# Two transformer blocks on one core: experts' norm applied in full, state-space evictions on ScalarE, four early expert units, rotation off Pool, cross-attention splits held to the softmax's end

## The chip, the cores and the metric

The program runs on one core of a Trainium2 chip. Its time is the device time of one execution in microseconds (us), the median of several. The engines are TensorE (PE, whose weight loads are shown apart as PEld), VectorE (DVE), ScalarE (ACT), GpSimd (POOL) and SyncE (SP, which issues most DMAs).

## What is computed

256 rows of 1024 float32 values pass through two blocks of two layers each, shortened from the reference:

```python
def first_block(x, ...):
    h = layer_norm(x, ln_in_g, ln_in_b)
    for l in range(2):
        mix = mixer_sublayer(h, ...)        # MLA + differential + forgetting attention, then w_out
        h = layer_norm(ALPHA * h + mix, ln1_g[l], ln1_b[l])
        ffn = grouped_moe(h, router_w, router_bias, w_gate[l], w_up[l], w_down[l])
        h = layer_norm(ALPHA * h + ffn, ln2_g[l], ln2_b[l])
    return h

def grouped_moe(h, ...):                    # 16 experts in 4 groups, best 2 of the best group
    scores = sigmoid(h @ router_w)
    ...
    for e in range(16):
        y = y + gates[:, e:e+1] * ((silu(h @ w_gate[e]) * (h @ w_up[e])) @ w_down[e])

def second_block(x, mem, ...):
    mem_k, mem_v = split(rms_norm(mem, mem_norm) @ mem_wkv, 2); mem_k = rms_norm(mem_k, mem_knorm)
    for i in range(2):
        x = x + 0.5 * swiglu(rms_norm(x, ffn1_norm[i]), ffn1_wi[i], ffn1_wo[i])
        h = rms_norm(x, mix_norm[i])
        x = x + (ssd_pool_mixer(h, ...) if i == 0 else swa_sink_attention(h, ...))
        x = x + memory_cross_attention(rms_norm(x, xattn_norm[i]), mem_k, mem_v, ...)
        x = x + 0.5 * swiglu(rms_norm(x, ffn2_norm[i]), ffn2_wi[i], ffn2_wo[i])
    return x
```

## The kernel before

The 256 rows are two tiles (`t` = 0, 1) of 128 partitions. Dense products are float32 by three passes (`mm3`, L483 to L485): each operand is split into a rounded high part and the rest, and high·high, high·low and low·high add up in PSUM. The experts' products (L1352 gate and up, L1386 down) and those of the memory (L1758) are single plain float32 passes.

**Weights.** `Stream` brings every weight once, in units of up to 1 MB, in the order of one list. A unit lands in one of two rings of tiles, `stage` (7) and `piece` (6). Dense weights are split on arrival, high on ACT (L161), low on DVE (L162); expert and memory units are "raw" and stay as they are. All these transfers are issued by SP, in order, each when its tile is free. Two expert units have places outside the rings, so that they can land before the experts begin: the first gate units of experts 0 and 1, in the main tiles `xl` and `m4`. `hold` and `go` keep splits of a named weight back and let some number of them go on.

**Order.** The program is laid out by a static scheduler: each engine gets one fixed list of instructions, formed from priorities, and `after(x)` keeps what follows behind `x`. So an instruction that waits holds up all behind it on its engine.

**The places that matter here.**
- *Norm before the experts* (`ln1`): a tile is normalised without its gain and bias (L581); they go into the router's weights (L1205, `rw`, `rc`), into the evictions of the gather (L1319 ACT, L1320 DVE) and, later, into the residual rows (`ln.gain`, L601 and L602). Each normalised tile is also split (L488 ACT, L489 DVE) for the gather.
- *Router*: transposes, 16 small matmuls (L1222), a sigmoid (L1225), some 20 small DVE instructions, then one-hot matrices (L1280) by which the rows of each expert are gathered with matmuls (L1318). Meanwhile PE runs one of the memory's products (L1758).
- *Experts*: eight pairs. Pair `pr` needs 8 gate and up units and 4 down units. Four groups of rows are gathered, group 0 ahead of the experts, group 1 in pair 0, groups 2 and 3 in pairs 2 and 4. `scatter` (L1401 on PE, L1403 on DVE) adds results to the rows. After the last pair, the next weights are split (4 of them, by `ws.go(4)`) and the second norm (`ln2`, L592 to L596) runs beside another product of the memory.
- *State-space mixer*: a four-tap convolution, decays, and per-head products; DVE evicts `upool` (L2059), `rows` (L2114), `bn` (L2145) and the gate `z` (L2189, a multiply out of PSUM).
- *Window attention*: key and value columns, then both halves of the queries, then the attention of the first half (scores L1980 and L1982, maxima L2000, exponentials, products), then that of the second.
- *Cross attention*: query product, norm of the queries, scores, softmax (L1831, L1841, L1856), products with the values, output product `xo`.

Of the kernel before, what the change touches and what calls it, by code (L numbers as in the profile page):

```python
# [16 lines left out]
P = 128  # L17
# [64 lines left out]
class Stream:  # L82
# [20 lines left out]
    def raw(self, key, ap, a, b, ring=0, slot=None):  # L103

        self.units.append(dict(ap=ap, a=a, b=b, left=1, tile=None, ring=ring, slot=slot, first=len(self.pieces)))
        u = len(self.units) - 1
        if not slot:
            self.use(key, u)
        return u

    def use(self, key, u):
        self.pieces.append(dict(key=key, u=u, raw=True, n=len(self.pieces)))

# [80 lines left out]
class LayerNorm:  # L194
# [8 lines left out]
    def tile(self, t):  # L203
        k = self.k
        if self.full:
            if t == 0:
                self.hi, self.lo = k.xt(self.tags[0]), k.xt(self.tags[1])
            k.ln_full(self.res, t, self.gb)
            self.copied = k.x_t(self.res[:, t, :], t, self.hi, self.lo, self.g)
            self.moved = k.moved  # L210
            return
        self.sqrt, self.last = k.ln_norm(self.res, t)
        if self.plain:
# [3 lines left out]
            if t == 0:  # L217
                self.hh = k.slot("m5", F32R).rearrange("p (t j f) -> p t j f", t=2, j=8)
                self.hl = k.slot("m2", F32R).rearrange("p (t j f) -> p t j f", t=2, j=8)
            v = self.res[:, t, :].rearrange("p (f j) -> p j f", j=8)  # L220
            self.parts = k.split(v, self.hh[:, t], self.hl[:, t])
        else:
            if t == 0:
                self.hi, self.lo = k.xt(self.tags[0]), k.xt(self.tags[1])
            self.copied = k.x_t(self.res[:, t, :], t, self.hi, self.lo, self.g, self.b)

# [41 lines left out]
class Kern:  # L268
# [62 lines left out]
    def plan(self):  # L331
        I, ws = self.I, self.ws
        for l in range(2):
# [11 lines left out]
            for c in range(2):  # L345
# [3 lines left out]
            early = lambda e, tag: ws.raw("gate", I["exp_w_gate"][l, e].rearrange("(p j) n -> p j n", j=8)[:, 0:4], 4, 512,  # L349
                                          slot=tag)  # L350
# [10 lines left out]

            def expert(key, ap, a, b):
                nonlocal n
                ws.raw(key, ap, a, b, n % (NSTAGE + NPIECE) % 2)
                n += 1

            for k in range(9):
                if k < 8:
                    for name in ("gate", "up"):
                        for j0 in (0, 4):  # L370
                            for e in (2 * k, 2 * k + 1):
                                if first:
                                    ws.use("gate", first.pop(0))
                                    continue
                                w = I["exp_w_" + name][l, e].rearrange("(p j) n -> p j n", j=8)
                                expert(name, w[:, j0:j0 + 4], 4, 512)
                if k > 0:
                    for c0 in (0, 2):
                        for e in (2 * k - 2, 2 * k - 1):
                            w = I["exp_w_down"][l, e].rearrange("(p c) n -> p c n", c=4)  # L380
                            expert("down", w[:, c0:c0 + 2], 2, 1024)
# [6 lines left out]
            mem(1024 * l + 512)  # L388
        self.plan2()

    def plan2(self):
        I, ws = self.I, self.ws
        for i in range(2):
# [15 lines left out]
            else:  # L409
                w = I["attn_wqkv_2"][0].rearrange("(p j) n -> p j n", j=8)  # L410
                self.plan_cols("qkv", w, 1024, 512)
                self.plan_cols("qkv", w, 0, 1024)
# [66 lines left out]
    def mm3(self, out, wst, wmv, first, last):  # L479
# [5 lines left out]
        return nc.tensor.matmul(out, al, bh, start=False, stop=last)  # L485
# [98 lines left out]
    def ln_full(self, res, t, gb):  # L584
# [10 lines left out]
        self.rsqrt1(r, mv[:, 1:2], 0)  # L595
        nc.vector.scalar_tensor_tensor(v, v, r, gb[1], op0=OP.mult, op1=OP.add)  # L596
# [221 lines left out]
    def mixer(self, l, norm, res, steps=None, moe=None):  # L818
# [182 lines left out]
        for k in range(2):  # L1001
            self.rope(qkd[:, k, :, :, 0:8], 4, 8, self.cos_d, self.sin_d, nc.gpsimd)
# [1289 lines left out]
```

## Time and profile before

| | |
|---|---|
| median of 3 runs (range) | 2002.53 us (2001.2 to 2002.54) |
| profiled execution | 2002.3 us |
| its span, first to last instruction | 2000.5 us |
| mean granted clock of TensorE, share of full speed | 0.986 |
| PE, PEld busy | 1935.0, 1458.6 us |
| DVE, ACT, POOL busy | 1127.0, 866.9, 58.0 us |
| moved by DMA | 453.39 MB, 227 GB/s over the span |

The span and the time differ by 1.8 us. PE is busy for 97% of the span, so at most 65.5 us of it are idle; the granted clock is 1 except in a few stretches, where the same matmuls take longer without PE being idle.

### The profile page before, as it was taken

To read this page: it belongs to the slowest core of one execution; us is meant where nothing else is said; L and a number is where in the kernel's file an instruction comes from. 1 tells how busy PE (TensorE), PEld (TensorE's weight loads), DVE (VectorE), ACT (ScalarE), POOL (GpSimd) and SP (SyncE) were. 2 spreads that over 40 slices of the span, in tenths; PEclk is the share of its full clock that TensorE was granted. 3 is DMA by queue.
4 is the path that set the end of the run, shared out by engine and by line. 5 is a ranking of instruction groups with operands and counts; after the bars stand their busy time and mean duration, and the time that the engine had idled before them with its cause. 6 is when DMAs were issued, how large, how long until landed. Compare 5 with 4: busy or idle time off the path is not lost.

```text
span 2000.5 us, 28009 instructions
## 1 busy us (share of the span) xinstructions
PE 1935.0 (97%) x11069; PEld 1458.6 (73%) x11069; DVE 1127.0 (56%) x2211; ACT 866.9 (43%) x1539; POOL 58.0 (3%) x119
## 2 busy tenths in 40 slices
PE   6999999999999998899999899999999999999999
PEld 6776433367864333599988887899989986778998
DVE  7775122167751221656579775655665567766554
ACT  6563110136631101455466555644454455556443
POOL 1110000000100000000001000000000000000000
PEclk9999999999999999999999999999999997999999
DMA  8456999973569999855564353455555543335550
GB/s 290 145 203 229 397 419 420 421 256 123 206 236 403 420 421 421 300 187 181 186 202 137 132 219 109 163 190 190 190 200 186 182 165 137 127 99 175 190 190 22
DMA packets 176044, 453.39 MB, mean 227 GB/s; under 512 B 11120, under 2 KB 106844, under 8 KB 149148
## 3 DMA queue, kind: packets, MB, share of 16 engines
q1 hardware_dynamic: 172044, 435.55, 59.1%
q0 software_dynamic: 3856, 15.91, 2.2%
q8 instruction: 91, 1.49, 0.3%
q14 instruction: 53, 0.43, 0.1%
HBM read 446.19 MB, written 5.24 MB: 226 GB/s over the span
## 4 chain that ended last, share of the span: by engine, by line
PE 56%; DMA 5%; DVE 3%; ACT 2%; issue 0%; POOL 0%; DVEq 0%; SPq 0%; POOLq 0%; ACTq 0%
PE mm L1623 7%; PE mm L1625 7%; PE mm L1624 7%; PE accb L485 5%; PE accb L484 5%; PE accb L483 4%; PE acca L485 4%; PE acca L484 4%; PE acca L483 4%; DMA piece<-in_exp_w_gate_dram 2%; DMA piece<-in_exp_w_down_dram 1%; DMA stage<-in_exp_w_down_dram 1%; DMA stage<-in_exp_w_up_dram 1%; DVE piece L162 1%; PE mm L1876 1%; PE mm L541 1%
## 5 line engine op out<-in xcount | busy, mean ns | idle before, releaser
L162 DVE TENSOR_TENSOR piece<-stage,piece 128x1024 fp32r<-128x1024 f32 (+3 forms) x439 | 513.8, 1179 | 240.9 <-ACT piece L161 239.3
L161 ACT ACTIVATE piece<-stage 128x1024 fp32r<-128x1024 f32 (+3 forms) x439 | 444.5, 1021 | 343.8 <-PE mm L1625 204.4
L1352 PE MATMUL mm<-stage,m 128*64 128x512 f32 x512 | 221.8, 595 | 0.0
L1352 PE MATMUL mm<-piece,m 128*64 128x512 f32 x480 | 215.1, 596 | 2.0 <-DMA piece<-in_exp_w_up_dram 2.0
L1623 PE MATMUL mm<-m,piece 128*128 128x256 f32 x736 | 207.0, 281 | 2.3 <-DVE m L2189 2.3
L1624 PE MATMUL mm<-m,piece 128*128 128x256 f32 x736 | 206.7, 281 | 0.0
L1625 PE MATMUL mm<-m,piece 128*128 128x256 f32 x736 | 206.6, 281 | 0.0
L1623 PE MATMUL mm<-xh,piece 128*128 128x256 f32 x576 | 163.1, 283 | 0.0
L1625 PE MATMUL mm<-xh,piece 128*128 128x256 f32 x576 | 163.0, 283 | 0.0
L1624 PE MATMUL mm<-xl,piece 128*128 128x256 f32 x576 | 162.9, 283 | 0.0
L484 PE MATMUL accb<-piece,m 128*128 128x512 f32 (+1 forms) x364 | 144.3, 397 | 0.0
L485 PE MATMUL accb<-piece,m 128*128 128x512 f32 (+1 forms) x364 | 143.7, 395 | 0.5 <-DVE m L493 0.5
L483 PE MATMUL accb<-piece,m 128*128 128x512 f32 (+1 forms) x364 | 143.1, 394 | 0.9 <-ACT m L950 0.7
L1623 PEld LDWEIGHTS mm<-m,piece 128*128 128x128 f32 x736 | 139.4, 189 | 4.6 <-issue 3.0
L1624 PEld LDWEIGHTS mm<-m,piece 128*128 128x128 f32 x736 | 139.3, 189 | 1.9 <-issue 0.3
L1625 PEld LDWEIGHTS mm<-m,piece 128*128 128x128 f32 x736 | 139.4, 189 | 0.0
L483 PE MATMUL acca<-piece,m 128*128 128x512 f32 (+1 forms) x348 | 138.2, 398 | 0.2
L485 PE MATMUL acca<-piece,m 128*128 128x512 f32 (+1 forms) x348 | 137.2, 396 | 0.5 <-DVE m L493 0.5
L484 PE MATMUL acca<-piece,m 128*128 128x512 f32 (+1 forms) x348 | 137.7, 396 | 0.0
L1352 PEld LDWEIGHTS mm<-stage,m 128*64 128x64 f32 x512 | 65.1, 137 | 76.4 <-issue 73.8
L1623 PEld LDWEIGHTS mm<-xh,piece 128*128 128x128 f32 x576 | 110.4, 192 | 1.3
L1624 PEld LDWEIGHTS mm<-xl,piece 128*128 128x128 f32 x576 | 110.4, 192 | 1.2
(567 smaller groups left out, 3535.8 us busy)
## 6 DMA issues: line engine op xcount, KB each, us to landing
stage<-in_ffn_wi_dram SPq DMA_DIRECT2D x88, 1024.0 KB, 5.5
stage<-in_ffn_wo_dram SPq DMA_DIRECT2D x44, 1024.0 KB, 5.4
stage<-in_exp_w_down_dram SPq DMA_DIRECT2D x38, 1024.0 KB, 18.6
stage<-in_exp_w_up_dram SPq DMA_DIRECT2D x34, 1024.0 KB, 11.2
stage<-in_exp_w_gate_dram SPq DMA_DIRECT2D x30, 1024.0 KB, 18.5
piece<-in_exp_w_gate_dram SPq DMA_DIRECT2D x30, 1024.0 KB, 17.9
piece<-in_exp_w_up_dram SPq DMA_DIRECT2D x30, 1024.0 KB, 15.0
piece<-in_exp_w_down_dram SPq DMA_DIRECT2D x26, 1024.0 KB, 16.8
```

The lines of the kernel that those rows point to most:

```text
L161: nc.scalar.activation(wh, src, AF.Copy)
L162: nc.vector.tensor_tensor(wl, src, wh.bitcast(F32), op=OP.subtract)
L483: nc.tensor.matmul(out, ah, bh, start=first, stop=False)
L484: nc.tensor.matmul(out, ah, bl, start=False, stop=False)
L485: return nc.tensor.matmul(out, al, bh, start=False, stop=last)
L541: self.moved = nc.tensor.transpose(p[:, k * P:(k + 1) * P], src[:, 4 * q + k:D:8], self.c["ident"])
L1352: mm = nc.tensor.matmul(o[64 * k:64 * k + 64, :], x[:, j, s:s + CAP], w[k][:, jj, :], start=(j == 0), stop=(j == 7))
L1623: nc.tensor.matmul(out, wh[:, j, :], hi[:, j, :], start=(j == 0), stop=False)
L1624: nc.tensor.matmul(out, wh[:, j, :], lo[:, j, :], start=False, stop=False)
L1625: nc.tensor.matmul(out, wl[:, j, :], hi[:, j, :], start=False, stop=(j == 7))
L1876: nc.tensor.matmul(po[:, k * P:(k + 1) * P], v[:, mc, h * 256 + cc * P:h * 256 + (cc + 1) * P], pt[t][:, (2 * h + mc) * P:(2 * h + mc + 1) ...
```

## The change

Seven edits, put in together:

1. `ln1` applies gain and bias at once (`ln_full`, two DVE passes of a tile, L594 and L596 of before). The premultiplied router weights, their bias row, the later `ln.gain`, and the row loads for it go; the gather's evictions become plain copies. Both tiles are split after the second one's norm.
2. Four expert units instead of two have places of their own (`xl`, `m4`, `m1`, `xh`), and they are other units, of later use: an up unit of expert 0 and three down units. The gathers of groups 1, 2 and 3 move to the end of pair 1 and into pairs 3 and 5. The second half of the memory's weights stands ahead of the next dense weight in the list.
3. The splits at the experts' end come later: two after the first tile of `ln2` is transposed, the rest after the second.
4. The rotation of the differential attention's queries and keys runs on DVE instead of POOL.
5. `upool`, `rows` and `bn` are evicted on ACT; `z` is copied out by ACT and multiplied by DVE in SBUF.
6. Cross attention finishes its query product bank by bank, starts the norm of each bank at its end, and puts the transposes and scores behind the last matmul; the splits of `xo` wait for the last normalised probabilities.
7. Window attention takes the first half of the queries, then keys and values, then the attention of the first half, then the second half of the queries.

```diff
-            first = [early(0, "xl")]
+            slots = {("up", 0, 4): "m4", ("down", 0, 0): "xl", ("down", 1, 0): "m1", ("down", 0, 4): "xh"}
...
+            early("down", 0, 0)
             self.plan_rows("w_out", I["w_out"][l].rearrange("(c p) n -> p c n", p=P), 8)
-            first.append(early(1, "m4"))
+            early("up", 0, 4)
...
+                    if n == NSTAGE + NPIECE - 2:
+                        early("down", 1, 0)
+                        early("down", 0, 4)
+            mem(1024 * l + 512)
...
-            mem(1024 * l + 512)
...
-            self.rope(qkd[:, k, :, :, 0:8], 4, 8, self.cos_d, self.sin_d, nc.gpsimd)
+            self.rope(qkd[:, k, :, :, 0:8], 4, 8, self.cos_d, self.sin_d, nc.vector)
...
-        ln = LayerNorm(self, res, ("ln1", l), None, ("xh",), plain=True)
+        ln = LayerNorm(self, res, ("ln1", l), self.load_gb(I["ln1_g"], I["ln1_b"], l), ("xh",), plain=True, full=True)
...
-                nc.tensor.matmul(o, n[:, j, t * P:(t + 1) * P], self.rw[l][:, j, :], start=False, stop=(j == 7))
+                nc.tensor.matmul(o, n[:, j, t * P:(t + 1) * P], self.rw[:, j, :], start=(j == 0), stop=(j == 7))
+        ws.free.append("xh")
...
-        at = gather(0)
-        with self.after(at):
-            ln.gain(rows)
+        gather(0)
...
-                if pr == 8:
-                    with self.after(state["silu"], state["tr"]):
-                        ws.go(4)
-            if pr == 0:
-                gather(1)
...
+            if pr == 1:
+                gather(1)
...
                 nxt.tile(0)
+            with self.after(*nxt.copied):
+                ws.go(2)
...
+        ws.hold("xo")
+        self.gemm_rows("xq", 8, lambda k: (hi[:, k, :], lo[:, k, :]), acc=rows(), done=chain, cuts=(2,), by_bank=True)
+        with self.after(self.last_mm):
+            for x in steps:
+                next(x, None)
...
+        with self.after(at[3]):
+            ws.go()
...
-        queries(0, 1)
+        attend(0, bias, "xl")
         queries(1, 1)
-        attend(0, bias, "xl")
...
-                nc.vector.tensor_scalar(u[:, t, b * 512:(b + 1) * 512], acc[t], r[:, t:t + 1], None, op0=OP.mult)
+                nc.scalar.activation(u[:, t, b * 512:(b + 1) * 512], acc[t], AF.Copy, scale=r[:, t:t + 1])
...
-            nc.vector.tensor_tensor(zs[:, ch, :], p[:, 0:256], rrow, op=OP.mult)
+            nc.scalar.activation(zs[:, ch, :], p[:, 0:256], AF.Copy)
+            nc.vector.tensor_tensor(zs[:, ch, :], zs[:, ch, :], rrow, op=OP.mult)
```

**Order on PE, first attention of the window layer.** Before: `accb` collects the last of the query product (high parts `m_16266`, low `m_16267`), `acca` the scores, `xh` holds normalised queries, `prob` probabilities.

```order
L485 MATMUL accb<-piece,m_16267 128x512
L1980 MATMUL acca<-m_16394,m_16392 128x128 x2
L1982 MATMUL acca<-m_16394,m_16392 128x256 x2
L1980 MATMUL acca<-m_16394,m_16392 128x128 x2
L1982 MATMUL acca<-m_16394,m_16392 128x256
L1967 MATMUL mm<-ident,xh 128x128 x8
L1982 MATMUL acca<-m_16394,m_16392 128x256
```

The same place after the change (`m_16227` and `m_16228` are the high and low parts, L1968 transposes keys, L1981 and L1983 are the scores):

```order
L1968 MATMUL mm<-ident,m_16354 128x128 x8
L487 MATMUL accb<-piece,m_16227 128x512
L488 MATMUL accb<-piece,m_16227 128x512
L489 MATMUL accb<-piece,m_16228 128x512
L1981 MATMUL acca<-m_16355,m_16353 128x128 x2
L1983 MATMUL acca<-m_16355,m_16353 128x256 x2
L487 MATMUL accb<-piece,m_16227 128x512
L488 MATMUL accb<-piece,m_16227 128x512
L1981 MATMUL acca<-m_16355,m_16353 128x128
L1983 MATMUL acca<-m_16355,m_16353 128x256
```

The scores of the first half, which came when the query product was over, now stand among the matmuls of the second half's queries.

**Order on DVE, end of the first layer's experts.** Before: the scatter's additions to `res`, splits of the next weight (L162) and the second norm (L592 on).

```order
L489 TENSOR_TENSOR xh<-acca,xh 128x512
L162 TENSOR_TENSOR piece<-stage,piece 128x768 x2
L489 TENSOR_TENSOR xh<-acca,xh 128x512
L162 TENSOR_TENSOR piece<-stage,piece 128x768 x2
L1403 SCALAR_TENSOR_TENSOR res<-res,mm 128x512 x4
L592 BN_STATS bnst<-res 128x6 x3
```

After the change:

```order
L494 TENSOR_TENSOR xh<-accb,xh 128x512 x2
L1387 SCALAR_TENSOR_TENSOR res<-res,mm 128x512 x4
L494 TENSOR_TENSOR xh<-acca,xh 128x512 x2
L1387 SCALAR_TENSOR_TENSOR res<-res,mm 128x512 x4
L597 BN_STATS bnst<-res 128x6 x3
```

No split stands between the scatter's additions and the norm any more.

**Order on DVE, the norm ahead of the router, second tile.** Before: norm (L581), split of that tile (L489), copy of the transposed tile that the router reads (L565, `xh`), and the router's first instruction.

```order
L531 TENSOR_TENSOR lnr<-sq_y,sq_t 128x1
L581 TENSOR_SCALAR res<-res,bnmv,lnr 128x1024
L489 TENSOR_TENSOR m_1639<-res,m_1638 128x1024
L565 COPY xh<-mm 128x4x128
L1227 TENSOR_TENSOR gbi<-gsc,rb 128x32
```

After the change:

```order
L536 TENSOR_TENSOR lnr<-sq_y,sq_t 128x1
L601 SCALAR_TENSOR_TENSOR res<-res,lnr,gv 128x1024
L494 TENSOR_TENSOR m_1686<-res,m_1685 128x1024 x2
L570 COPY xh<-mm 128x4x128
L1215 TENSOR_TENSOR gbi<-gsc,rb 128x32
```

The split of the first tile, which ran while the second was being summed, now stands with the other ahead of the router's copy.

## Rows read from the trace of the kernel before

**Rows 1.** PE's waits, experts of layer 0: what for, us in total, times, longest.

```profile
PE mm L1401 <- DVE res L1403: 2.9, 4, 1.8
...
PE mm L1352 <- DMA piece<-in_exp_w_up_dram: 1.3, 1, 1.3
```

**Rows 2.** PE's waits, experts of layer 1.

```profile
PE mm L541 <- DVE sq_y L530: 4.0, 1, 4.0
PE accb L1386 <- DMA stage<-in_exp_w_down_dram: 2.1, 2, 1.3
PE accb L1758 <- DMA stage<-in_mem_wkv_dram: 1.4, 1, 1.4
```

**Rows 3.** Stretches: length, busy PE, PEld, DVE, ACT, POOL, granted clock, DMA share, GB/s.

```profile
175.00:200.00 25.00, 25.00 (x147) 16.04 (x147) 11.34 (x21) 7.56 (x12) 1.09 (x2) 0.93 0.46 147
...
375.00:400.00 25.00, 21.73 (x91) 7.47 (x88) 3.88 (x7) 3.28 (x5) 0.28 (x3) 1.00 1.01 421
```

**Rows 4.** Stretches at the experts' ends, layers 0 and 1.

```profile
412.50:417.50 5.00, 4.65 (x8) 2.35 (x9) 5.00 (x10) 0.30 (x1) 0.00 (x0) 0.66 1.07 373
...
822.50:827.50 5.00, 4.34 (x13) 3.01 (x14) 3.81 (x12) 4.07 (x11) 0.00 (x0) 0.66 1.07 385
```

**Rows 5.** Timeline of DVE, end of layer 0's experts: start, us, line, operation.

```profile
408.04 1.83 DVE L162 TENSOR_TENSOR piece<-stage,piece 128x768 fp32r<-128x768 f32 x2
...
416.97 1.27 DVE L594 SCALAR_TENSOR_TENSOR res<-res,bnmv,gv 128x1024 f32<-128x1024 f32 x1
```

**Rows 6.** PE's waits from the state-space mixer to the cross attention.

```profile
PE tp L2175 <- DVE prob L2166: 3.4, 2, 2.3
PE mm L1623 <- DVE m L2189: 2.3, 1, 2.3
PE mm L1837 <- DVE m L1831: 1.6, 1, 1.6
```

**Rows 7.** Stretches of the state-space mixer.

```profile
1075.00:1100.00 25.00, 24.99 (x162) 19.71 (x161) 23.82 (x57) 14.96 (x23) 5.28 (x6) 1.00 0.29 98
...
1112.50:1120.00 7.50, 5.24 (x34) 4.88 (x30) 5.83 (x12) 1.58 (x4) 0.00 (x0) 0.54 0.63 225
```

**Rows 8.** Timeline of DVE, end of the state-space mixer.

```profile
1109.52 1.22 DVE L162 TENSOR_TENSOR piece<-stage,piece 128x1024 fp32r<-128x1024 f32 x1
...
1111.78 1.41 DVE L2059 TENSOR_SCALAR m<-accb,rms_r 128x512 f32<-128x512 f32 x2
```

**Rows 9.** PE's longest wait in the window layer.

```profile
PE acca L1980 <- DVE wnm L2000: 4.5, 2, 4.2
```

**Rows 10.** Stretches of the window layer: query projection, attention's first half, its second half.

```profile
1650.00:1665.00 15.00, 15.00 (x70) 12.31 (x69) 14.34 (x25) 8.00 (x10) 0.53 (x1) 1.00 0.76 262
1677.00:1703.00 26.00, 25.24 (x85) 16.03 (x85) 12.95 (x69) 12.19 (x44) 0.00 (x0) 0.50 0.08 32
1703.00:1719.00 16.00, 16.00 (x91) 10.05 (x89) 11.20 (x60) 7.74 (x29) 0.00 (x0) 0.99 0.01 2
```

**Rows 11.** Timeline of DVE, norm ahead of the router, layer 0.

```profile
162.67 0.81 DVE L581 TENSOR_SCALAR res<-res,bnmv,lnr 128x1024 f32<-128x1024 f32 x1
165.62 2.02 DVE L489 TENSOR_TENSOR m<-res,m 128x1024 fp32r<-128x1024 f32 x1 [2.15 <-ACT m L488]
```

**Rows 12.** Timeline of ACT, same place and the gather.

```profile
161.76 1.28 ACT L504 ACT_TABLE_LOAD   x1
163.06 0.20 ACT L504 ACTIVATE warm<-eps 128x1 f32<-128x1 f32 x1
...
169.44 0.20 ACT L1225 ACTIVATE gsc<-tp 128x32 f32<-128x32 f32 x1 [3.26 <-PE tp L1222]
176.12 0.56 ACT L1319 ACTIVATE m<-mm,gcol 128x256 f32<-128x256 f32 x1 [6.49 <-PE mm L1318]
```

**Rows 13.** Groups of instructions, 100 to 106 us: busy us, mean ns.

```profile
L1205 PE MATMUL tp<-rw,gcol 128*1 128x16 f32 x32 | 1.1, 176 | 0.0
```

**Rows 14.** The rotation's line 771: count, duration in ns least/median/most.

```profile
L771 DVE TENSOR_TENSOR m<-gv x2: 425/425/425, 67.4 to 472.1; 128x256 f32<-128x256 f32 x2
```

More of the change, by code (lines that the diff above doesn't have):

```diff
@@ L103, in raw @@
     def raw(self, key, ap, a, b, ring=0, slot=None):
-        self.units.append(dict(ap=ap, a=a, b=b, left=1, tile=None, ring=ring, slot=slot, first=len(self.pieces)))
+        first = max((p["n"] + 1 for p in self.pieces if not p.get("raw")), default=0)
+        self.units.append(dict(ap=ap, a=a, b=b, left=1, tile=None, ring=ring, slot=slot, first=first))
         u = len(self.units) - 1
@@ L204, in tile @@
         k = self.k
[L205 to L212, printed above, removed]
+        self.sqrt, self.last = k.ln_full(self.res, t, self.gb) if self.full else k.ln_norm(self.res, t)
         if self.plain:
@@ L217, in tile @@
             if t == 0:
[L218 to L221, printed above, removed]
+                return
+            self.hh = k.slot("m5", F32R).rearrange("p (t j f) -> p t j f", t=2, j=8)
+            self.hl = k.slot("m2", F32R).rearrange("p (t j f) -> p t j f", t=2, j=8)
+            with k.after(self.sqrt, self.last):
+                for i in range(2):
+                    v = self.res[:, i, :].rearrange("p (f j) -> p j f", j=8)
+                    k.split(v, self.hh[:, i], self.hl[:, i])
         else:
@@ L797, in block1 @@
         self.ws.start(5)
-        next(moe)
+        self.moe_consts()
         self.ws.start()
@@ L808, in block1 @@
         for l in range(2):
-            ln = self.mixer(l, ln, res, *([] if l else [steps, moe]))
+            ln = self.mixer(l, ln, res, *([] if l else [steps]))
             if self.stop == 1 + 2 * l:
@@ L816, in block1, with mixer @@
         return res, ln
-    def mixer(self, l, norm, res, steps=None, moe=None):
+    def mixer(self, l, norm, res, steps=None):
         nc, I, c, ws = self.nc, self.I, self.c, self.ws
@@ L1210, in moe @@
         n, hh, hl = ln.n, ln.hh, ln.hl
-        x = self.slot("m1")
-        rows = [x[:, 0:D], x[:, D:2 * D]]
-        for r, v in zip(rows, (I["ln1_g"], I["ln1_b"])):
-            nc.gpsimd.dma_start(r, bcast_rows(v, D, l * D))
+        ws.free.append("m1")
         sc = self.sm(32, "gsc")
@@ L1357, in gate_or_up @@
                 ws.release(2)
+            state["last"] = mm
             return o
@@ L1842, in queries, with chain @@
                          nc.vector.tensor_scalar(qv[:, :, 1, :], pv[:, :, 1, :], g[:, 1:2], None, op0=OP.mult))
-            sc[t] = [self.acc(t), self.acc(t)]
-            for h in range(4):
-                for cc in range(2):
-                    nc.tensor.matmul(sc[t][h // 2][:, (h % 2) * 256:(h % 2) * 256 + 256], qT[:, 2 * h + cc, ts[t]],
-                                     kT[:, 2 * h + cc, :], start=(cc == 0), stop=(cc == 1))
+            for b in banks:
+                s = self.acc(t)
+                sc.setdefault(t, []).append(s)
+                for h in range(2):
+                    for cc in range(2):
+                        nc.tensor.matmul(s[:, h * 256:h * 256 + 256], qT[:, 4 * b + 2 * h + cc, ts[t]],
+                                         kT[:, 4 * b + 2 * h + cc, :], start=(cc == 0), stop=(cc == 1))
+        normed, steps = [], []
+        def chain(*x):
+            steps.append(queries(*x))
+            next(steps[-1])
         def attend(t):
```

200 lines of the change are left out of this document (93 added, 107 removed).

## The prediction

> **What bounds the kernel now.** I read the page first: PE is busy for 1935.0 of 2000.5 us, so the edits can win back only the 65.5 us in which it is idle and the stretches in which its clock is low; its own work hardly changes. Then the waits of PE and the table of stretches, stage by stage, for where these lie. Four places carry most of what the diff touches.
>
> *Experts.* In the later pairs DMA is the limit: its share is 1.01 at 421 GB/s, and PE is idle for 3.27 of 25 us (25.00 - 21.73) [rows 3]. A unit of 1 MB (1.049 million bytes) takes 2.49 us at that rate. PE waits for weights at single places: 1.3 us in layer 0 [rows 1], 2.1 us and, for the memory's weights, 1.4 us in layer 1 [rows 2].
>
> *Experts' ends.* DVE makes four splits ahead of the last additions to `res`, the first two 1.83 us [rows 5]. PE waits up to 1.8 us for `res` in layer 0 [rows 1] and 4.0 us for the second norm in layer 1 [rows 2], and in either layer a stretch of 5 us has a mean clock of 0.66 [rows 4], that is, part of it at 1.2 GHz.
>
> *State-space mixer.* DVE is busy for 23.82 of 25 us [rows 7]; PE then waits 3.4 and 2.3 us for it [rows 6], and has a mean clock of 0.54 for 7.5 us [rows 7].
>
> *Window attention.* PE waits 4.2 us for a maximum on DVE [rows 9], and its clock is at 0.50, the 1.2 GHz level, for the next 26 us, the whole first half. PE counts as busy there; the same work of the second half takes 16 us at 0.99 [rows 10].
>
> **The change part by part.** The sum is made against the profiled execution, 2002.3 us, which is 0.2 under the median of the three runs.
>
> *Early units.* Between 175 and 200 us DMA's share is 0.46 [rows 3], so some 13.5 us of it stand free: the rings are full, and no tile is released before the experts begin. Two more units outside the rings take 2 × 2.49 = 5.0 us from that free time, and all later weights arrive 5.0 us sooner. The three shown waits for weights (1.3 + 2.1 + 1.4 = 4.8 us) go. SP issues in order, so if it stood at `xh`, which comes free only after the router's matmuls, the units behind it would stand too; they need ring tiles that come free later still. Lower end: nothing, if PE's pace and DMA's are so close that the wait comes back in a later pair. Upper end: all of the 3.27 us of the late stretch [rows 3] in both layers and 1.4 for the memory, 8. I take **5**.
>
> *Gathers later.* Group 1 is gathered at the end of pair 1, and pair 2's gate product needs it: its last eviction of 0.56 us [rows 12] may stand open there, once in a layer. Groups 2 and 3 stay a product ahead. 0 to -2, I take **-1**.
>
> *Experts' ends.* Without the splits on DVE, the norm of layer 0 comes some 3.6 us sooner (two times 1.83 [rows 5]). To win: the waits of 1.8 [rows 1] and 4.0 us [rows 2], and what the low clock costs, 5 × (1 - 0.66) = 1.7 us in either layer [rows 4]: 9.2 at most. The splits now stand after the transposes, where DVE needs about 0.9 us for each; the next dense product can be held by the third and fourth. Lower end 2, I take **6**.
>
> *Norm in full, router.* 32 small matmuls in the records (16 instructions) go, 1.1 us [rows 13], under full load of PE: **1**. On the chain to the router, L581 (0.81 us [rows 11]) becomes a pass like L594 (1.27 [rows 5]), and the first tile's split now stands before the router's copy, 2.02 us on DVE [rows 11]. DVE had waited 2.15 us for ACT at that place [rows 11], so the added split partly fills a wait; by that the sigmoid, now at 169.44 [rows 12], comes some 2.0 to 2.5 us later. The cover is the memory's product; where it ends, PE waits. The four bias matmuls and 9 us of `ln.gain` on DVE that go were hidden under it. I take **-1.5** for both layers, with -5 (all 2.5 us in each) and 0 as ends.
>
> *Rotation.* 12 instructions in each layer, at most 0.425 us each on DVE (a row of four times the width [rows 14]), 5.1 us at most, under dense products and on a DVE that is nearly idle there: **0**.
>
> *State-space evictions.* `upool` leaves DVE with 1.41 us for two of its four [rows 8], so 2.8 in all, `rows` and `bn` with a little more. For `z` DVE keeps a multiply of the same size, and only its wait for PE moves to ACT, which was busy for 1.58 of 7.5 us [rows 7]. To win: waits of 5.7 us [rows 6], and the low clock, 7.5 × (1 - 0.54) = 3.4 us [rows 7], 9 together; lower end 1, because `prob` on DVE (L2166) stays behind a split of 1.22 us [rows 8]. I take **5**, what the shorter DVE list explains and a part of the clock.
>
> *Cross attention.* The query chain of one bank lies under the other's matmuls: the wait of 1.6 us [rows 6], which the second layer shows too, 3.2 together, 5 with smaller ones. Against it, the `xo` splits begin only when the probabilities are normalised; if two of 1.22 us [rows 8] are late in each layer, that is -5. I take **2.5**.
>
> *Window attention.* The second half's queries stand among the scores of the first half, so PE has a dense product to run while DVE and ACT do the softmax. If the first half goes like the second, 26 us become 16 [rows 10], and the 4.2 us [rows 9] go as well: 14.2. ACT must change its table twice more between exponentials and a square root: 2 × 1.28 us [rows 12] = 2.6, on a chain that PE waits for. DVE also gets the second half's splits and norms. Ends 0 (the clock stays low) and 17 (4.2 and half of 26). I take **10**.
>
> A rule speaks against the last step. The Trainium skill (ScalarE: Activation LUTs, "What ACT_TABLE_LOAD costs") gives 2.66 us for a change of table, the load and a drain behind it. This trace disagrees: the ACTIVATE at 163.06 starts 0.02 us after the load has ended [rows 12]. By the page the two changes would cost 5.3 us in place of 2.6, and the sum would be 2.7 us smaller.
>
> Sum: 5 - 1 + 6 + 1 - 1.5 + 0 + 5 + 2.5 + 10 = 27; 2002.3 - 27 = 1975.3, so **1975 us**.
>
> **The rivals.**
> *The window attention keeps its low clock in the first half.* For it: PE, DVE and ACT hand each head pair on, and the clock stayed at 0.50 through all of it [rows 10]. Against it: the second half, which is made of the same steps, ran at 0.99. Then only the wait of 4.2 is won, less 2.6: 1975 + 10 - 1.6 = 1983 us.
>
> *The experts give nothing and the router takes its upper price.* The waits for weights come back in later pairs (0 for 5), and the chain ends 2.5 us late in each layer (-5 for -1.5): 1975 + 5 + 3.5 = 1984 us.
>
> *Slower.* The projection that now fills the first half is drawn into the low clock with it: PE has gaps while it waits for DVE, the clock is at 0.50 from the first score to the last, the second half too. Then the first half wins nothing (10), the second takes 32 in place of 16 us [rows 10] (16), and the projection, 48 matmuls (8 weight chunks, 2 tiles, 3 passes) at 15.00 / 70 = 0.214 us [rows 10], takes 20 in place of 10 us (10): 1975 + 36 = 2011 us. It decides when 27 of these 36 us come about.
>
> *Better.* All ends of experts' tails, mixer and window come in: 1975 - 3 - 4 - 7 = 1961 us.
>
> **How the numbers follow.** Forecast 58% (1966 to 1982 for itself), low clock in the first half 17%, experts and router 12%, slower 6%, better 7%. The first three and a part of the better one hold 8 in 10 and more between 1962 and 1984 us; the upper end of 1992 is for the splits of `xo`, which could cost 7.5 us more than I took. A measurement of this kernel tells about 0.2%, 4 us, from no change: faster than 1998.5 us is 0.90, between that and 2006.5 is 0.04 (the rivals of smaller gain together), slower 0.06.
>
> **What the profile after would show.** Early units: no wait for expert or memory weights, DMA's share in the stretch before the experts above 0.46. Ends: `res` additions without a split before them, no wait on the norm in layer 1, clock 1 there. Mixer: PE's waits on L2166 and `z` shorter, clock near 1 up to 1120. Window: granted clock 1 through the first half, no wait of some 4 us, the stage 10 us shorter. Router: the sigmoid some 2 us later after the norm, PE's wait there under 1.5 us. Wrong it would be if the clock of the window attention stayed at 0.50, if PE waited for `xo` pieces in both layers, or if the gather of group 1 held up pair 2 by more than a microsecond.

## The result

The changed kernel took 1955.57 us (median of four runs, 1954.59 to 1958.93) against 2002.53; the ratio is 0.977 with a 95% interval of 0.9753 to 0.9787. That is 47 us, where 27 were forecast, and 6 us under the low end of the range. The profiled execution took 1954.59 us, its span is 1952.8.

The page of the changed kernel, busy time of each engine (us, share of the span, instructions):

```profile
PE 1910.2 (98%) x11029; PEld 1445.3 (74%) x11029; DVE 1121.6 (57%) x2236; ACT 866.1 (44%) x1558; POOL 46.7 (2%) x93
```

PE is idle for 42.6 us (1952.8 - 1910.2) where it was idle for 65.5, and its busy time fell by 25 us, although it lost only 40 short records: most of that part is time at the low clock. The mean clock rose from 0.986 to 0.997, so the span lost some 28.0 us to the low clock before (2000.5 × 0.014) and 5.9 after (1952.8 × 0.003), an estimate that counts idle time at the low clock too.

The waits of PE of the changed kernel, whole span (us in total, times, longest):

```profile
PE mm L546 <- DVE res L586: 7.2, 1, 7.2
...
PE mm L1152 <- DVE prob L2017: 3.7, 2, 3.1
PE mm L546 <- DVE sq_y L535: 2.6, 2, 1.3
...
PE acca L1370 <- DMA piece<-in_exp_w_down_dram: 0.3, 1, 0.3
```

Of the waits in [rows 1, 2, 6, 9], those for expert weights are down to 0.3 us, those of the state-space mixer are gone, the norm at the experts' ends costs 1.3 us in each layer, and the window layer has a new one of 3.1 us.

Where the time went is read best from the start or end of PE instructions that both programs have. Lengths in us of the profiled executions:

| stage | before | after | won |
|---|---|---|---|
| start to the first attention's value product | 80.6 | 76.5 | 4.1 |
| to the memory product beside the router | 76.0 | 72.5 | 3.5 |
| to the first gate product, layer 0 | 28.4 | 27.6 | 0.8 |
| gate and up products, layer 0 | 202.2 | 195.4 | 6.8 |
| to the end of the second memory product (experts' end) | 42.7 | 38.1 | 4.6 |
| mixer of layer 1 | 127.6 | 127.7 | -0.1 |
| to the first gate product, layer 1 | 28.2 | 28.8 | -0.6 |
| gate and up products, layer 1 | 201.9 | 195.6 | 6.3 |
| experts' end, layer 1 | 45.0 | 38.6 | 6.4 |
| to the state-space products per head | 257.9 | 257.5 | 0.3 |
| to the first cross attention's transposes | 123.8 | 116.4 | 7.4 |
| to the second one's (with the window layer) | 551.7 | 543.5 | 8.2 |
| to the last matmul | 230.5 | 230.3 | 0.2 |

Each number is rounded by itself. The two stages that end at a cross attention's transposes hold the wait in front of these: 1.6 us in the first one before the change [rows 6], as much in the second, nothing after it; that part of the 7.4 and of the 8.2 us belongs to the cross attention's edit.

The stretches of the window layer after the change (columns as in [rows 3]):

```profile
1630.00:1640.00 10.00, 9.57 (x56) 6.61 (x56) 7.76 (x40) 7.69 (x22) 0.00 (x0) 1.00 0.01 5
1640.00:1650.00 10.00, 7.62 (x36) 4.68 (x34) 8.38 (x30) 8.25 (x25) 0.00 (x0) 1.00 0.31 105
1650.00:1660.00 10.00, 8.14 (x44) 5.71 (x46) 6.88 (x25) 6.75 (x17) 0.00 (x0) 0.83 0.30 107
1660.00:1670.00 10.00, 8.95 (x49) 5.38 (x49) 7.07 (x42) 5.35 (x21) 0.00 (x0) 1.00 0.01 2
```

The clock stays up but for a part of one stretch, and PE is idle for 5.7 us of 40.

DVE at the end of layer 0's experts, which answers to [rows 5]:

```profile
392.42 2.62 DVE L1387 SCALAR_TENSOR_TENSOR res<-res,mm 128x512 f32<-128x512 f32 x4
394.95 1.87 DVE L597 BATCH_NORM_STATS2 bnst<-res 128x6 f32<-128x512 f32 x3
...
404.72 1.83 DVE L164 TENSOR_TENSOR piece<-stage,piece 128x768 fp32r<-128x768 f32 x2
```

The norm follows the additions at once, and the splits come behind it.

### The profile page after: what moved, and what is told of

Same layout as the page of the kernel before. It is cut to its first block, busy times and chain, and to the rows that moved or that the text cites. A ratio compares the mean times of both kernels' runs of the same rounds, so it can differ in the third digit from the quotient of the medians.

```text
span 1952.8 us, 27956 instructions
## 1 busy us (share of the span) xinstructions
PE 1910.2 (98%) x11029; PEld 1445.3 (74%) x11029; DVE 1121.6 (57%) x2236; ACT 866.1 (44%) x1558; POOL 46.7 (2%) x93
## 4 chain that ended last, share of the span: by engine, by line
PE 59%; ACT 3%; DVE 2%; DMA 2%; issue 1%; ACTq 0%; DVEq 0%; SPq 0%
PE mm L1606 8%; PE mm L1607 8%; PE mm L1605 8%; PE accb L487 4%; PE accb L489 4%; PE accb L488 4%; PE acca L489 4%; PE acca L488 4%; PE acca L487 4%; PE mm L1335 2%; DMA piece<-in_exp_w_down_dram 1%; ACT piece L163 1%; DMA piece<-in_exp_w_gate_dram 1%; PE acca L1370 1%; PE mm L1869 1%; PE accb L1370 1%
## 5 line engine op out<-in xcount | busy, mean ns | idle before, releaser
L1335 PE MATMUL mm<-stage,m 128*64 128x512 f32 x528 | 231.4, 600 | 0.0
L489 PE MATMUL accb<-piece,m 128*128 128x512 f32 (+1 forms) x364 | 143.8, 396 | 0.5 <-DVE m L498 0.5
L489 PE MATMUL acca<-piece,m 128*128 128x512 f32 (+1 forms) x348 | 137.3, 396 | 0.7 <-DVE m L498 0.7
## 6 DMA issues: line engine op xcount, KB each, us to landing
stage<-in_exp_w_up_dram SPq DMA_DIRECT2D x32, 1024.0 KB, 11.1
```

Source lines behind the costliest of these rows:

```text
L489: self.last_mm = nc.tensor.matmul(out, al, bh, start=False, stop=last)
L1335: mm = nc.tensor.matmul(o[64 * k:64 * k + 64, :], x[:, j, s:s + CAP], w[k][:, jj, :], start=(j == 0), stop=(j == 7))
```

## Experiments

Eighteen kernels ran. Ten take one edit out of the changed kernel, or part of it; two try to improve it; six put edits into the kernel before. Times are medians; the lengths are those of the table's stages in the profiled run of each. Many stages that no edit touches repeat within 0.3 us. The start and the stretch from the memory product to the first gate product repeat within some 1.1 us, the window layer within 1.4, and the experts' products are the least steady: 195.4 to 198.2 us for the same code in layer 0, where the clock from 175 to 187.5 us is 1.00 in the changed kernel's profile and 0.73 in that of e4, and 195.3 to 196.7 in layer 1. So up to 2.8 of the 6.8 us won in layer 0 can be the clock's.

### The start: two small loads (e2_gcol_back)

```diff
+        self.gain_columns(1)      # ln1_g, ln1_b, on SP, not used
         self.rw = self.cp.tile([P, 8, 16], F32, name="rw")
```

> The changed kernel with the two small loads of ln1 gain and bias columns put back at the start (32-byte pieces, 8 KB each; loaded and not used). Theory S1, these loads held up the weights behind them on the DMA rings, and the 4 us by which the first 80 us became shorter come from there: 3 to 5 us longer by the first attention, 1959 us. Theory S2, the order of VectorE's work at the start changed with the rest, and the loads cost nothing: under 1 us, 1955.5 us.

1963.62 us, 8.1 longer; the first stage took 83.0 us against 76.5. That is more than S1 foresaw, and not by its path. The timeline of ACT, this run:

```profile
31.31 0.19 ACT L904 ACTIVATION_READ_ACCUMULATOR m<-m 128x1 f32 x1
34.13 0.37 ACT L1714 ACTIVATE m<-mm,gcol 128x128 f32<-128x128 f32 x1 [2.64 <-PE mm L1707]
...
36.32 3.05 ACT L163 ACTIVATE piece<-stage 128x776 fp32r<-128x776 f32 x4
```

The same of the changed kernel:

```profile
29.78 0.19 ACT L904 ACTIVATION_READ_ACCUMULATOR m<-m 128x1 f32 x1
29.87 1.58 ACT L163 ACTIVATE piece<-stage 128x776 fp32r<-128x776 f32 x2
```

With the loads in the program, the scheduler puts two splits of the first weights behind an eviction for which ACT stands 2.64 us; without them they come first. The row above each is 1.5 us later in this run, which is the most that SP and the rings can have cost up to there. The rest of the 6.5 us goes with another fixed order of ACT, and with the clock: from 60 to 72 us it is 0.86 in this run, as in the kernel before, and 1.00 in the changed one. How much each carries is not shown.

### Other loads of the start (v1_late_consts, f1_before_gcol)

```diff
-        self.moe_consts()
         self.ws.start()
...
         self.load_consts()
+        self.moe_consts()
```

> The changed kernel with two other small loads of the start, the router's weights and bias, moved behind the loads of the first norm and the constants on SP. If every small load ahead of them makes the first norm late as the gain and bias columns of ln1 did (3 us on the loads, 7 us on the start for two), 2 to 5 us shorter: 1952 us. If only what made these two special (their 32-byte pieces) counts, the same: 1955.5 us.

1955.5 us, the first stage 77.5: no gain. The kernel before, with the four loads of `moe_consts` behind the norm's rows in the same way:

> The kernel before with the ln1 gain and bias columns and the router's constants loaded behind the first norm's rows and the constants on SP, nothing else. If their place ahead of those rows made the start slow, the first attention begins some 4 to 6 us sooner: 1997 us. If the pieces themselves slow the weights wherever they stand, no gain: 2001.5 us.

2002.64 us, ratio 1.0005 (0.9995 to 1.0015); first stage 81.2. In that run ACT has the early splits, as after the change, and PE waits 3.5 us for the memory's norm instead. So the place of the loads is not the cause, and no single cause of the start's 4.1 us is shown: it belongs to one fixed order that came out well.

### The experts: early units and gathers

**e1_two_early**:

```diff
-            slots = {("up", 0, 4): "m4", ("down", 0, 0): "xl", ("down", 1, 0): "m1", ("down", 0, 4): "xh"}
+            slots = {("up", 0, 4): "m4", ("down", 0, 0): "xl"}
```

> The changed kernel with two early expert units (those in xl and m4) in place of four; the gathers stay where the change put them. Theory A, DMA paces the experts as a whole, so each megabyte loaded ahead shortens the stage by its own 2.49 us, whether or not a wait is shown at one place: 5 us longer in each layer, in all 1965 us. Theory B, the one of the prediction, only the shown waits for weights come back: 5 us in both layers together, 1960 us. Theory C, the later gathers won the time: no change, 1955.5 us.

1960.41 us, 4.8 longer, which is theory B's number; theory A is too high. Gate and up products take 197.8 and 197.9 us. In layer 0 that is a length that the same code has elsewhere (up to 198.2); in layer 1 the products are 2.3 us longer and the experts' end 0.7. The mechanism of B is not shown by it: the waits for expert weights are 1.4 us in this run and 0.3 in the changed kernel, 1.1 us for a loss of 4.8.

**e8_no_early**:

```diff
+            slots = {}
```

> The changed kernel with no expert unit outside the rings. The experts' products took 195.5 to 198 us in a layer with four early units and 197.8 with two. If DMA paces them, two units fewer cost 2 x 2.49 = 5 us in each layer against two: 203 us, 1970 us in all. If PE's own work now paces them, nothing: 198 us, 1960 us.

1972.46 us; 200.9 and 204.7 us, 3.1 and 6.8 more than with two. The first two units are worth about what DMA's pace says (9.9 of 10 us), and the second two about half (4.8); why less is not shown.

**e9_gate_early**: the same number as e1, of other use.

```diff
-            slots = {("up", 0, 4): "m4", ("down", 0, 0): "xl"}
+            slots = {("gate", 0, 0): "xl", ("gate", 1, 0): "m4"}
```

> The changed kernel with two early units, and those that the kernel before had: the first gate units of experts 0 and 1, the first to be used. Against the run with two early units of later use (experts' products 197.8 and 197.9 us) this tells whether it is the kind of unit. Theory R, units outside the rings that are used first keep the ring tiles full for longer, so SP's stream of weights starts again later and the experts, paced by DMA, take 201 to 202 us in each layer: 8 us over that run, 1968 us. Rival, the kind makes no difference, and the experts became shorter by the moved gathers: 198 us, 1960 us.

1965.75 us, 5.3 more than e1; 198.2 and 199.8 us. R foresaw 201 to 202 and 8 us. In the profiled execution the kind of unit carries only 0.4 and 1.9 us of the products, but that execution, at 1962.04 us with a mean clock of 0.998, is 3.7 us under the median, and its clock is 1.00 all through the products, which e1's is not (0.86 from 175 to 187.5 us). So the use of the units is worth 2.3 us at the least and 5.3 by the medians.

**e10_gathers_back**: e9 and the gathers at their old places.

```diff
+            if pr == 0:
+                gather(1)
-            if pr == 2:
+            if pr == 1:
                 ptr.append(self.slot("xl", F32R).rearrange("p (a n) -> p a n", a=8))
...
-            if pr in (3, 5):
+            if pr in (2, 4):
                 gather(pr // 2 + 1)
```

> The run with the two gate units as the early ones, and also the gathers and the transposed one-hot matrices where the kernel before had them (group 1 in pair 0, the matrices in pair 1, groups 2 and 3 in pairs 2 and 4). Theory G: work of 3 to 5 us that stands on PE early in the experts holds up the release of ring tiles, hence the stream of weights; the experts take 202 us in each layer as before the change, against 198 and 200: 1970 us. Rival: the places of the gathers do not matter, 198 to 200 us, 1965 us.

1971.25 us, 5.5 more than e9; 201.7 and 203.5 us: 3.5 and 3.6 more than e9, and about the length of before. The stretches after the first gate product of layer 0, e9 and then this run:

```profile
176.00:186.00 10.00, 10.00 (x52) 3.99 (x54) 0.33 (x2) 1.88 (x2) 0.00 (x0) 1.00 0.48 157
186.00:196.00 10.00, 10.00 (x48) 3.13 (x46) 1.07 (x3) 0.00 (x0) 0.00 (x0) 1.00 1.00 418
```

```profile
176.00:186.00 10.00, 10.00 (x46) 3.86 (x45) 0.33 (x2) 0.00 (x0) 0.00 (x0) 0.83 0.39 140
186.00:196.00 10.00, 10.00 (x63) 6.08 (x63) 1.76 (x5) 3.20 (x6) 0.00 (x0) 1.00 0.67 234
```

With the gather of group 1 in pair 0, PE uses up expert tiles later, DMA stands still for a third of the second stretch, and the stream of weights is late to its end. PE is busy throughout these two stretches, so no wait shows the loss there. It shows later: PE's waits for expert weights are 8.0 us in this run and 2.7 in e9, here the first two of this run.

```profile
PE accb L1367 <- DMA stage<-in_exp_w_down_dram: 2.6, 2, 1.3
PE mm L1332 <- DMA piece<-in_exp_w_up_dram: 1.4, 2, 0.7
```

The clock is not the same in the two profiles: 0.83 in this run's first stretch where e9 has 1.00, and the same again in layer 1. Up to 1.7 us in each layer (10 × 0.17) can be the clock's, so the gathers carry between 3.7 us (7.1 - 3.4) and 7.1 in the stages; the medians say 5.5.

**f3_before_gathers**: the same lines the other way round, alone, in the kernel before.

> The kernel before with the later places of the gathers and one-hot transposes, nothing else. Theory G, they let the stream of weights start sooner: 3.5 to 4.5 us less in each layer, 1994 us, with no dip of DMA between 187 and 196 us. Rival, only together with early units of later use: under 2 us, 2000 us.

1998.66 us, 3.7 less, ratio 0.9987 (0.9977 to 0.9997). 0.8 and 3.0 us in the products, 1.2 won and 1.7 lost behind them. In layer 1 the clock is at 1.00 all through the products in this run and in before, so those 3.0 us are none of the clock's. G holds in part: alone, with the first gate units outside the rings, the later gathers bring 3.7 us, where G foresaw 7 to 9.

### The experts' ends (e4_tail_back, f4_before_tail, f5_before_tail_mem, f6_tail_gathers)

```diff
+                if pr == 8:
+                    with self.after(state["silu"], state["tr"]):
+                        ws.go(4)
...
-            with self.after(*nxt.copied):
-                ws.go(2)
```

> The changed kernel with four splits of the next weight put back ahead of the last scatter of the experts. Theory T, the splits on VectorE made the scatter and the second norm late: 3.6 us in layer 0 and 4.7 in layer 1 on VectorE come back, 1961 to 1964 us, with waits for res and for the norm. Rival, the ends became shorter because the last expert weights land sooner: under 2 us, 1957.5 us at most.

1969.0 us, 13.4 longer; the ends take 42.8 and 44.2 us in place of 38.1 and 38.6: 10.3 us. DVE in this run, and the longest wait of PE at each end:

```profile
401.34 1.27 DVE L599 SCALAR_TENSOR_TENSOR res<-res,bnmv,gv 128x1024 f32<-128x1024 f32 x1
402.53 3.56 DVE L164 TENSOR_TENSOR piece<-stage,piece 128x768 fp32r<-128x768 f32 x4
```

```profile
PE mm L546 <- DVE sq_y L535: 4.8, 1, 4.8
```

```profile
PE mm L546 <- DVE res L601: 5.9, 1, 5.9
```

Theory T stands for the changed kernel. The reverse in the kernel before (the same lines, with the signs changed):

> The kernel before with the splits at the experts' end behind the norm's transposes, nothing else. Theory T, 10.8 us came back when the splits were put back in the changed kernel, and the same is won here: 1991 us, with no splits ahead of the last additions. Rival, half of it hangs on the weights that land sooner in the changed kernel: 1996 us.

2006.18 us, ratio 1.003 (1.0016 to 1.0044): 0.3% slower, not faster. The timeline of DVE shows why:

```profile
413.13 2.69 DVE L162 TENSOR_TENSOR piece<-stage,piece 128x768 fp32r<-128x768 f32 x3
415.74 1.87 DVE L592 BATCH_NORM_STATS2 bnst<-res 128x6 f32<-128x512 f32 x3
```

The splits are ahead of the norm all the same. In the list of weights of before, the next dense weight stands ahead of the memory's second half, and taking a weight brings the splits of all ahead of it. So this edit needs the other one that reads as a detail. Both together in the kernel before:

```diff
+            mem(1024 * l + 512)
             if l == 0:
                 w = I["w_in"][1].rearrange("(p j) n -> p j n", j=8)
...
-            mem(1024 * l + 512)
```

> The kernel before with the splits at the experts' end moved and the memory's second half ahead of the next dense weight in the list. If the list's order is what was missing: 4.6 us in layer 0 and 6.5 in layer 1 less from the last gate and up product to the end of the memory's product (42.7 and 45.1 us before), no split ahead of the norm, 1991 us. If not, no more than 2 us: 2001 us.

2000.11 us, ratio 0.9988 (0.997 to 1.0006). The ends take 39.3 and 39.2 us: 3.4 and 5.8 won, 9.2 of the 11.1 expected, and the list's order is what was missing. The time shows less of it: in the profiled run the stretch to the per-head products, the one from there to the first cross attention and the one from the second to the end are 1.1 to 1.7 us longer each, in code that is the same, and the ten runs spread from 1990.3 to 2003.8 us, with mean clocks of 0.989 to 0.984. With the later gathers on top:

> The same with the later gathers added. If gathers and ends add up, 3 to 5 us less than that run, 1987 us; if the later gathers need early units of later use, no difference.

1991.37 us, ratio 0.9944 (0.9924 to 0.9963). Products of 201.2 and 200.6 us and ends of 38.1 and 40.4: 2.2 us less than f5 in these four stages, where 3 to 5 were expected if the two add up. The rest of the 8.7 us between the medians is not from the edit's stages; both kernels' runs spread by 9 us and more.

### The state-space evictions (e5_ssd_dve)

The four evictions back as `nc.vector` instructions; the last of them:

```diff
-            nc.scalar.activation(zs[:, ch, :], p[:, 0:256], AF.Copy)
-            nc.vector.tensor_tensor(zs[:, ch, :], zs[:, ch, :], rrow, op=OP.mult)
+            nc.vector.tensor_tensor(zs[:, ch, :], p[:, 0:256], rrow, op=OP.mult)
```

> The changed kernel with the four state-space evictions (upool, rows, bn, z) back on VectorE. Theory M, they are what shortened the stretch from the per-head products to the cross attention by 7.4 us: 6 to 8 us longer, 1962 us, the stretch 123 to 124 us in place of 116.4. Rival, the stretch became shorter through the cross attention's new order, which ends it: under 3 us.

1965.27 us; the stretch to the cross attention takes 123.1 us in place of 116.4, the one before it 1.3 more. The waits of before [rows 6] are back to the tenth:

```profile
PE tp L2175 <- DVE prob L2166: 3.4, 2, 2.3
PE mm L1605 <- DVE m L2189: 2.3, 1, 2.3
```

M holds: 8.0 us in the two stages, of which 5.7 are these waits. The low clock is back too: 0.53 from 1082 to 1093 us.

### Cross attention (e6_xattn_back)

```diff
-        ws.hold("xo")
-        self.gemm_rows("xq", ..., done=chain, cuts=(2,), by_bank=True)
+        self.gemm_rows("xq", ..., done=chain, cuts=(2,))
```

> The changed kernel with the cross attention in the old form: no hold of the xo splits, the query product not finished bank by bank, transposes and scores not put behind its last matmul. Theory X, PE's waits in this stage went from 2.5 to 1.5 us in a layer, so 2 us are lost: 1957.5 us. Rival, the stage also took something from the state-space and window stages before it (both end in the query product): 4 to 8 us, 1960 to 1963 us.

1961.87 us, 6.3 longer. In the first cross attention 1.8 us are lost in front of the transposes and 1.8 behind them, where the clock is 0.57 from 1180 to 1184 us; in the second some 2 to 3 in front, in a stage that varies by 1.4 us by itself, and 0.2 behind. About 6 us, the rival's amount; its reason, that the stages before the cross attention end with its query product, fits the parts in front.

### Rotation (e7_rope_pool, f2_before_rope)

```diff
-            self.rope(qkd[:, k, :, :, 0:8], 4, 8, self.cos_d, self.sin_d, nc.vector)
+            self.rope(qkd[:, k, :, :, 0:8], 4, 8, self.cos_d, self.sin_d, nc.gpsimd)
```

> The changed kernel with the rotation of the differential attention back on Pool. Theory of the prediction: no change, 1955.5 us within 1. Rival, the transposes behind the rotation were late, and the stretch from the first attention to the memory product (72.5 us after, 76.0 before) is 1 to 2.5 us longer, in both layers.

1967.43 us, 11.9 longer: 4.4 us in layer 0 and 8.3 in layer 1. PE's longest wait there, layers 0 and 1:

```profile
PE mm L1013 <- POOL m L777: 2.3, 2, 1.5
```

```profile
PE mm L1013 <- POOL m L777: 4.1, 2, 3.4
```

> The kernel before with the rotation on VectorE, nothing else. Theory O, the list of PE covers the rotation in the kernel before and does not in the changed one without this edit: no gain, 2000 to 2002 us, with the 127.6 us between the memory products kept. Rival, the rotation on Pool is 8 us late in each order: 1990 us.

2004.25 us, ratio 1.0009 (0.9997 to 1.002): nothing, as theory O says. In the kernel before, PE has no wait for POOL at the transposes in either layer; in the changed one, with the rotation on POOL, it has. The two waits are 6.4 us of the 12.7; two stretches of 3.4 us at a clock of 0.50 in layer 1 (from 497.7 and from 528.4 us) are a further part. So the edit wins nothing over before and yet can't be left out.

### The window layer (e3_swa_back, v2_sqrt_late)

```diff
-                for c0 in (0, 1024, 512):
-                    self.plan_cols("qkv", w, c0, 512)
+                self.plan_cols("qkv", w, 1024, 512)
+                self.plan_cols("qkv", w, 0, 1024)
...
-        attend(0, bias, "xl")
+        queries(0, 1)
         queries(1, 1)
+        attend(0, bias, "xl")
```

> The changed kernel with the window layer in the old order (keys and values, both halves of the queries, then attention). Theory W, the new order is worth the 8 us by which this stage became shorter: 1963.5 us, and the clock at 0.50 again through the first half. Rival, the clock was low only because of how the stage fell in time, and the order is worth less than 3 us: under 1958.5 us, clock near 1.

1958.95 us, 3.4 longer; from the first cross attention to the second 547.0 us in place of 543.5. The wait of 4.2 us is back, and so is the low clock, and still the stage is 4.7 us shorter than before. The old order stands in before, in this run and in f1 to f6, with the same wait and the same instructions; what differs is how long the clock stays low. It differs between runs of this one program too: two took 1956.8 and 1957.0 us at a mean clock of 0.993, the other two 1960.9 and 1961.4 at 0.990. Two stretches from the wait on, the kernel before and f3_before_gathers:

```profile
1672.00:1697.00 25.00, 20.08 (x76) 12.47 (x73) 15.64 (x71) 14.40 (x44) 0.00 (x0) 0.58 0.23 83
1697.00:1722.00 25.00, 25.00 (x122) 16.41 (x120) 16.09 (x85) 12.95 (x50) 0.53 (x1) 0.87 0.05 12
```

```profile
1672.00:1697.00 25.00, 20.08 (x94) 13.07 (x93) 18.10 (x82) 17.17 (x55) 0.00 (x0) 0.73 0.25 85
1697.00:1722.00 25.00, 25.00 (x142) 16.98 (x142) 18.98 (x85) 15.58 (x50) 0.72 (x2) 1.00 0.13 43
```

PE is idle for 4.92 us in both, but gets through 198 and 236 matmuls. From the first scores to the transposes of the cross attention that is 94.3 us in one and 87.9 in the other; in e3 it is 89.8. With e3's stage moved to either end of that range, an estimate, the new order wins under 2 us against an old one with a short low clock, and 8 against one with a long low clock.

The other run keeps the new order and ties the norm of the second half's queries to the last exponential of the first half (`outs["exp"]`):

```diff
-        queries(1, 1)
+        queries(1, 1, (outs["exp"],))
...
+            with self.after(*behind):
+                self.rsqrt(ss.rearrange("p t h -> p (t h)"), ss.rearrange("p t h -> p (t h)"), 1, scale=1.0 / 64)
```

> The changed kernel with the square root of the second half's queries put behind the last exponentials of the first half, so that ScalarE does not change its table between them. If the two table loads of 1.28 us stand on the chain that PE waits for, 1.5 to 3 us shorter: 1953 us. If the second half then starts later by as much, the same; if its norm has become the chain, up to 3 us longer.

1965.04 us, 9.5 longer: the third case, at three times its price. The stretches of its first half:

```profile
1650.00:1660.00 10.00, 5.79 (x26) 3.79 (x25) 7.47 (x24) 6.62 (x22) 0.00 (x0) 0.74 0.33 120
...
1670.00:1680.00 10.00, 7.58 (x27) 4.95 (x26) 4.65 (x23) 4.36 (x20) 0.00 (x0) 0.60 0.00 1
```

PE is idle for 4.2 us of the first stretch and 2.4 of the other, and the clock falls. The two table loads were the smaller price. They stand on ACT in the changed kernel like this:

```profile
1649.80 1.28 ACT L516 ACT_TABLE_LOAD   x1
1651.10 0.31 ACT L516 ACTIVATE sq_t<-swasq,eps 128x16 f32<-128x16 f32 x1
```

No run beat the changed kernel: v1_late_consts equals it.

## Why the prediction was wrong

*Experts' products: the step that failed.* The sum took 5 us for the early units and -1 for the later gathers, 4 together. The products became 13.0 us shorter, and e10, which turns number and use of the units and the places of the gathers back, costs 15.7 us by the medians: 4.8 for two units less (e1), 5.3 more for units that are used first (e9), 5.5 more for the gathers. So the 5 us for two more units came out about right, and two other things failed. That the early units are of later use had no term at all; it is worth 2.3 to 5.3 us. And the gathers had the wrong sign: I gave them -1, for an eviction that may stand open, where they carry 3.7 to 7.1 us, because they had kept PE from releasing tiles while the rings were full. [rows 3] had shown the sign of it: a DMA share of 0.46 ahead of the saturated stretch. I read it as room for more units instead of as a stream that starts late.

*The waits as a price.* I counted three waits for weights, 4.8 us. The whole span of the kernel before lists 7.7 us, with these rows beside those of [rows 2] (the 2.0 include the 1.3 of [rows 1]):

```profile
PE mm L1352 <- DMA piece<-in_exp_w_up_dram: 2.0, 2, 1.3
...
PE acca L1386 <- DMA piece<-in_exp_w_down_dram: 1.0, 1, 1.0
...
PE accb L1386 <- DMA piece<-in_exp_w_down_dram: 1.0, 1, 1.0
...
PE acca L1386 <- DMA stage<-in_exp_w_down_dram: 0.2, 1, 0.2
```

And even these are not the price. They went down to 0.3 us, PE's idle time in the products fell from 11.2 to 4.8 us, and the products became 13.0 shorter; the rest is spread over records that count as busy. Where DMA paces a stage, the length of the stage is the measure.

*Experts' ends: mechanism right, size off.* 11.1 us where I took 6 with 9.2 as the most. The upper end counted only the first waits and the low clock. That the edit hangs on the list's order (f4, f5) I had not seen; I had booked the memory's place in the list as a wait of 1.4 us.

*Start: left out.* The sum had nothing for it but 1.1 us of small matmuls; the first two stages gave 7.6. In the first, the fixed order of ACT moved with the loads that went (e2), and the cause of its 4.1 us stays open. In the second, the 3.5 us won hang on the rotation: with it back on POOL the stage is 4.4 us longer (e7), though alone it wins nothing there (f2).

*Norm and router: nearly right.* 0.8 won and 0.6 lost where -1.5 was taken; the sigmoid comes 13.2 us after the start of the memory product against 12.9 (162.20 and 169.44 us), and PE shows no wait. The 0.6 lost in layer 1 can be the clock's, which is 0.66 from 563 to 573 us after the change.

*State-space evictions: right.* 5.8 us (7.4 less the cross attention's 1.6; 8.0 in reverse) for 5, under the upper end of 9.

*Cross attention: right in sign.* About 6 us in reverse for 2.5; the held `xo` splits were never late.

*Rotation: right against the kernel before* (f2: nothing), but wrong for the changed order, where the edit is worth 11.9 us (e7).

*Window attention: right in size, not in cause.* 8.2 us for 10, of which 1.6 are the cross attention's, clock up as foreseen, and a new wait of 3.1 us. That the size came out near is in part luck. The old order varies by 6.4 us with the clock, so the 26 us at 0.50 [rows 10] were one case of it, and 16 the model of another. The two changes of table, costed at 2.6 us, are there. The next ACTIVATE starts 0.02 us after the load, so the drain that the Trainium skill adds to the load (ScalarE: Activation LUTs, "What ACT_TABLE_LOAD costs") is not seen here either.

What stays open: why one fixed order of the start is 4 us better than others (loads moved either way do not show it), what makes the low clock last, and how the experts' gain splits to the microsecond, since medians and stages differ by up to 3 us.

## What to carry to other kernels

In a stage that DMA paces, look for when the stream starts and what keeps tiles from being released, not only for the waits that are named; work that can wait belongs behind the first releases. An edit that moves an instruction behind another does so only if the list it stands in lets it: splits that are forced by taking a later weight come first whatever they were tied to. And where a static scheduler forms the order, single edits do not add up: the seven reversals (e2 to e7 and e10) cost 3 to 16 us each and 68 together, where the whole change won 47, and four edits put in alone changed the time by 0, +2, -4 and +4 us, the first two within what was measured as no change.

## What was not expected of the hardware

After the same idle time of 4.92 us in the same 25 us, with the same instructions, the mean clock over the 50 us was 0.73 in one run and 0.87 in another, and the stage 6.4 us longer in the first: what one idle gap costs is not fixed by its length.
